# Seven-product gates in a hybrid encoder block: seven of eight feature tiles of the gate projection as 2x2 block products, the merged sum kept in fp32 and split in the w_out stage

## The chip, the core and the metric

The kernel runs on one core of a Trainium2 chip. The metric is the device time of one execution in microseconds, as a median over several runs; a second number, the span of one profiled execution with its trace, says where the time lies. The core has a matrix engine (PE, with its weight loads, PEld), a vector engine (DVE), a scalar engine (ACT), GpSimd (POOL), and SyncE (SP), which issues most of the DMAs. Each engine takes its instructions strictly in the order of its own queue, and waits for others by semaphores.

## The reference

One layer of an encoder, 512 positions of width 1024, all in float32 (cut to what matters):

```python
n = rms_norm(h, norm_mix_pre)
proj = einsum('bsd,de->bse', n, w_in)          # columns: gMLP u | v | q | k | v | gates
z_gmlp, q, k, v, gates = split(proj)
y_a = gmlp_spatial_gating(gelu(z_gmlp), ...)   # [512, 512]
y_b = mixture of three dilated window attentions(q, k, v)   # [512, 512]
g_all = sigmoid(gates + b_gate)                # gates: [512, 2048]
g_a, g_b = g_all[..., :1024], g_all[..., 1024:]
merged = g_a * (y_a @ w_branch_a) + g_b * (y_b @ w_branch_b)
h = h + rms_norm(merged @ w_out, norm_mix_post)
n2 = rms_norm(h, norm_mlp_pre)
h = h + rms_norm(square(relu(n2 @ w_up)) @ w_down, norm_mlp_post)
```

## The kernel before, in words

Every product of two float32 matrices is made of three matmuls: an operand is split into a high part (`hi`, a copy rounded by ACT into the matmul type) and a low part (`lo`, the rest, a subtraction on DVE), and `mm3` (L83-87) adds hi x hi, hi x lo and lo x hi. Such a split is `wsplit` (L70-77, ACT at L75, DVE at L76) or `split_into` (L79-81, ACT at L80, DVE at L81). A 1024x128 column block of weights is 128x1024 on the chip.

The program is a row of stages on PE: the q, k, v projections and attention of four heads; the gMLP's v and u projections (the attention of the last head, `attend(3)`, runs between them; its matmuls at L407-409 are the last readers of the split values `v0h`, `v0l`); the gates and branches (L494-514); the w_out product (L566-604); the up projection (L642-726); the down projection.

Gates and branches, before: eight feature tiles `d` of 128 columns. For each, the two gate projections are 24 matmuls of 512 columns each (8 blocks of the contraction, three matmuls each, weights x the normalised input `nh`, `nl`), a sigmoid on ACT (L506) reads each from PSUM; the two branch products are 12 matmuls of 512 columns each (`ybh`, `ybl` the attention output, `yah`, `yal` the gMLP output). DVE multiplies each with its gate (L512), adds the two (L513), and the sum is split at once into `mh` and `ml` (L514), which w_out reads. Weights come as 1 MB DMAs for two tiles (`gw`, `bw`).

The gates of the first tile run interleaved with the last attention head and the gMLP's u stage, because the scheduler that orders the instructions fills PE's queue with what it expects to be ready. The order of every engine's queue is fixed when the program is built. Buffers are taken from pools: a new tile waits for the last reader of the tile whose slot, or whose memory, it takes. PSUM has eight banks, with tags in `psA` ("acc" 4 banks, "S" 2, "T" 1, "y" 1) for the stages up to the gates and in `psB` ("acc" 4, "tp" 4) behind them; a bank of `psB` waits for the last reader of the bank of `psA` that lies there.

In the up projection the kernel already has a seven-product scheme (L654-726): two output tiles of 128 features and two halves of 256 positions form a 2x2 block product, computed with seven block products instead of eight, each of 12 matmuls of 256 columns (L687); sums of the weights (L670, L671, L676) and of the moving operand (L656-659) are made on DVE and split, and the results are put together from PSUM on DVE and ACT (L708-722).

Of the kernel before, what the change touches and what calls it, by code (L numbers as in the profile page):

```python
# [36 lines left out]
def block_kernel(ctx: ExitStack, tc: tile.TileContext, x, norm_mix_pre, w_in, b_gate, ln_v_gain, ln_v_bias,  # L37
# [157 lines left out]
    spacer(right, 160, "yedge")  # L195
# [230 lines left out]
    gpool = pool(gst, "gpool")  # L426
# [40 lines left out]

    for g2 in range(2):
# [15 lines left out]

    gst.close()
    attn.close()

    mst = ExitStack()
    mpool = pool(mst, "mpool")
    mh = mpool.tile([P, KD, S], F32R, name="mh")  # L490
    ml = mpool.tile([P, KD, S], F32R, name="ml")
    gp = ExitStack()
    gapool = pool(gp, "gapool", bufs=2)
    for d2 in range(4):  # L494
        raws = [wload([KD, 2 * P], lambda r: [(r, fcols(w_in, COL_G + br * D + d2 * 2 * P, KD, 2 * P))], "gw") for br in range(2)]
        rawb = wload([2, 4, 2 * P], lambda r: [(r[:, br], w[:, d2 * 2 * P:(d2 + 1) * 2 * P].rearrange("(k p) c -> p k c", p=P))
                                               for br, w in enumerate((w_branch_a, w_branch_b))], "bw")
        for j in range(2):
            d = 2 * d2 + j
            sl = slice(j * P, (j + 1) * P)  # L500
            tmp = []
            for br in range(2):
                wh, wl = wsplit(raws[br][:, :, sl])
                ps = feature_tile(wh, wl, KD, nhn, nln)
                sg = gapool.tile([P, S], F32, name=f"sg{br}")
                nc.scalar.activation(sg, ps, AF.Sigmoid, bias=cols[:, br * 8 + d:br * 8 + d + 1])  # L506
                tmp.append(sg)
            for br in (1, 0):
                bh, bl = wsplit(rawb[:, br, :, sl], gapool, tag=f"b{br}")
                yh, yl = ((yah, yal), (ybh, ybl))[br]  # L510
                pb = feature_tile(bh, bl, 4, yh, yl)
                nc.vector.tensor_tensor(tmp[br], pb, tmp[br], op=ALU.mult)  # L512
            nc.vector.tensor_tensor(tmp[0], tmp[0], tmp[1], op=ALU.add)  # L513
            split_into(mh[:, d], ml[:, d], tmp[0])  # L514
# [6 lines left out]
    spacer(back, 224, "nedge")  # L521
# [9 lines left out]
    KH = KD // 2  # L531
# [30 lines left out]
    def w_out_mm(t, k, hf, wh, wl):  # L562
        ts_ = slice(t * P, (t + 1) * P)
        mm3(accs[t][hf], (mh[:, k, ts_], ml[:, k, ts_]), (wh[:, halves[hf]], wl[:, halves[hf]]), k == 0, k == KD - 1)
# [44 lines left out]

    wback = pool(back, "wback", bufs=5)  # L610
# [43 lines left out]
    fe, fo = n2f[:, 0:KD:2], n2f[:, 1:KD:2]  # L654
    A, B = slice(0, 256), slice(256, 512)
    nc.vector.tensor_tensor(fe[:, :, A], fe[:, :, A], fe[:, :, B], op=ALU.subtract)  # L656
    nc.vector.tensor_tensor(fe[:, :, B], fo[:, :, B], fe[:, :, B], op=ALU.subtract)
    nc.vector.scalar_tensor_tensor(fo[:, :, B], fe[:, :, A], -1.0, fo[:, :, B], op0=ALU.mult, op1=ALU.subtract)
    nc.vector.scalar_tensor_tensor(fo[:, :, A], fo[:, :, B], -1.0, fo[:, :, A], op0=ALU.mult, op1=ALU.subtract)
    nt = {}  # L660
    for nm, src in ((2, fo[:, :, B]), (1, fe[:, :, A]), (3, fe[:, :, B]), (4, fo[:, :, A])):
        nt[nm] = (n2_tile(), n2_tile())
        split_into(*nt[nm], src)
# [3 lines left out]
    def prep(i):  # L667
        raw = raw_up(i).rearrange("p (j h) (r c) -> p j (h r) c", h=2, r=2)
        s = upool.tile([P, KH, 4, P], F32, name="s", bufs=1)
        nc.vector.tensor_tensor(s[:, :, 0:4:2], raw[:, :, 1:3], raw[:, :, 0:1].to_broadcast([P, KH, 2, P]), op=ALU.add)  # L670
        nc.vector.tensor_tensor(s[:, :, 3], s[:, :, 2], raw[:, :, 1], op=ALU.add)  # L671
        s12 = split_back(s[:, :, 2:4], [KH, 2, P])
        ar = split_back(raw[:, :, 1:3], [KH, 2, P])
        a12 = [upool.tile([P, KH, P], F32R, name="a12" + z) for z in "hl"]
        split_into(*a12, raw[:, :, 3])
        nc.vector.tensor_tensor(s[:, :, 1], s[:, :, 3], raw[:, :, 3], op=ALU.add)  # L676
        s34 = split_back(s[:, :, 0:2], [KH, 2, P])
        pick = lambda g, m: [z[:, :, m] for z in g]
        return {1: pick(ar, 0), 2: a12, 3: pick(s34, 1), 4: pick(ar, 1), 5: pick(s12, 0), 6: pick(s12, 1), 7: pick(s34, 0)}

    moving = {1: nb[0, 0], 2: nb[1, 0], 3: nb[1, 1], 4: nt[4], 5: nt[1], 6: nt[2], 7: nt[3]}

    def product(n, ps, w, first):
        (wh, wl), (bh, bl) = w[n], moving[n]
# [129 lines left out]
```

## Time and profile before

| | |
|---|---|
| median of 3 runs | 833.03 us (832.04 to 834.82) |
| profiled execution | 832.47 us |
| its span in the trace | 830.7 us, so 1.8 us lie around the span |
| PE busy | 812.6 us, 98% |
| DVE busy | 491.6 us, 59% |
| ACT busy | 348.6 us, 42% |
| gates and branches, on PE | about 306 to 432.9 us |
| w_out | 432.9 to 478.4 us |
| up projection, seven-product part | 510.3 to about 652 us |

How to read it: the page gives the busy time of each engine and the chain of work that ended last, followed back through what released each step. A timeline row has the start in us, the duration in us, the engine, the line, the operation, output and inputs by the program's names, the shape, and how many such rows in a row were put together (x2); in square brackets stands how long the engine had been idle before it, and what ended that idle time. The durations of neighbouring rows overlap by a little, since engines are pipelined; the spacing of starts is what a row costs in a dense stretch. A row of the windows table gives a stretch, its length, the busy time and number of instructions of PE, weight load, DVE, ACT and POOL, then the granted PE clock (1.00 is full), the DMA share and GB/s.

### The profile page before, as it was taken

How to read it: one execution, taken by the hardware profiler on the slowest of the kernel's cores; microseconds unless marked ns; L12 is line 12 of the kernel's file. 1: busy time of each engine (PE TensorE's matmuls, PEld its weight loads, DVE VectorE, ACT ScalarE, POOL GpSimd, SP SyncE). 2: the span in 40 equal slices, each digit the busy share in tenths (PEclk: the TensorE clock that was granted, in tenths of full speed). 3: DMA queues.
4: the chain of work that ended last, by engine and by line, in shares of the span. 5: the costliest groups of instructions: out<-in, count | busy, mean ns of one | idle time of the engine just before them, and what ended most of it. 6: DMA issues, size and time to landing. Idle time of an engine off the chain costs nothing.

```text
span 830.7 us, 10935 instructions
## 1 busy us (share of the span) xinstructions
PE 812.6 (98%) x4371; PEld 706.5 (85%) x4371; DVE 491.6 (59%) x831; ACT 348.6 (42%) x561; POOL 83.0 (10%) x81
## 2 busy tenths in 40 slices
PE   7999999999999999999999989999999999999997
PEld 5899888888888778888888879999999888888885
DVE  6422788978875647433332589989787533333324
ACT  6322243435344353332322566666666533223311
POOL 2100113232215200000000220000000000000000
PEclk9999999999999999999999989999999999999999
DMA  9433233222214134431413241443333722222202
GB/s 297 143 102 84 70 100 102 77 76 81 73 51 124 56 101 136 144 102 51 152 51 102 101 153 52 130 123 104 102 102 128 253 101 102 91 77 89 99 1 101
DMA packets 70373, 86.90 MB, mean 105 GB/s; under 512 B 2034, under 2 KB 57490, under 8 KB 70323
## 3 DMA queue, kind: packets, MB, share of 16 engines
q1 hardware_dynamic: 67810, 77.67, 29.7%
q0 software_dynamic: 2512, 8.54, 3.0%
q8 instruction: 34, 0.56, 0.3%
q14 instruction: 17, 0.13, 0.0%
HBM read 82.01 MB, written 4.19 MB: 104 GB/s over the span
## 4 chain that ended last, share of the span: by engine, by line
PE 96%; ACT 2%; DMA 1%; DVE 1%; issue 0%; SPq 0%; DVEq 0%; POOLq 0%; ACTq 0%
PE pf L87 12%; PE pf L86 11%; PE pf L85 11%; PE pacc L687 11%; PE pd L85 9%; PE pd L87 9%; PE pd L86 9%; PE ptp L687 5%; PE pv L85 4%; PE pv L86 4%; PE pv L87 4%; PE pu L85 1%; PE pu L87 1%; PE pu L86 1%; PE py L413 1%; PE psb L313 1%
## 5 line engine op out<-in xcount | busy, mean ns | idle before, releaser
L87 PE MATMUL pf<-nh,lo 128*128 128x512 f32 x352 | 138.2, 393 | 0.0
L86 PE MATMUL pf<-nl,hi 128*128 128x512 f32 x352 | 138.1, 392 | 0.0
L85 PE MATMUL pf<-nh,hi 128*128 128x512 f32 x352 | 137.8, 392 | 0.0
L687 PE MATMUL pacc<-n,hl 128*128 128x256 f32 x840 | 104.2, 279 | 0.0
L687 PEld LDWEIGHTS pacc<-n,hl 128*128 128x128 f32 x840 | 100.8, 188 | 0.3 <-ACT hl L80 0.2
L85 PE MATMUL pd<-hl,hh 128*128 128x512 f32 x224 | 87.1, 390 | 1.0 <-ACT hh L80 1.0
L86 PE MATMUL pd<-hl,hh 128*128 128x512 f32 x224 | 87.2, 389 | 0.0
L87 PE MATMUL pd<-hl 128*128 128x512 f32 x224 | 86.0, 389 | 0.0
L85 PEld LDWEIGHTS pf<-nh,hi 128*128 128x128 f32 x352 | 66.1, 188 | 13.6 <-issue 0.2
L87 PEld LDWEIGHTS pf<-nh,lo 128*128 128x128 f32 x352 | 66.1, 188 | 13.5 <-issue 0.2
L86 PEld LDWEIGHTS pf<-nl,hi 128*128 128x128 f32 x352 | 66.1, 188 | 13.3
L81 DVE TENSOR_TENSOR hl<-hid,hh 128x512 fp32r<-128x512 f32 x28 | 19.3, 693 | 80.3 <-ACT hh L80 78.9
L254 POOL TENSOR_TENSOR sw<-sw,rope 32x512 f32<-32x512 f32 x24 | 42.2, 1760 | 175.1 <-DVE sw L252 158.0
L80 ACT ACTIVATE hh<-hid 128x512 fp32r<-128x512 f32 x28 | 17.6, 631 | 93.2 <-PE pd L86 93.2
L85 PE MATMUL pv<-hi,nh 128*128 128x512 f32 x128 | 51.4, 405 | 0.9 <-ACT nh L80 0.9
L86 PE MATMUL pv<-lo,nh 128*128 128x512 f32 x128 | 51.6, 403 | 0.0
L87 PE MATMUL pv<-hi,nl 128*128 128x512 f32 x128 | 51.5, 403 | 0.0
L85 PEld LDWEIGHTS pd<-hl,hh 128*128 128x128 f32 x224 | 42.0, 188 | 10.3 <-ACT hh L80 1.4
L87 PEld LDWEIGHTS pd<-hl 128*128 128x128 f32 x224 | 42.0, 188 | 8.8
L86 PEld LDWEIGHTS pd<-hl,hh 128*128 128x128 f32 x224 | 42.0, 188 | 8.6
L81 DVE TENSOR_TENSOR hl<-dnw,hl 128x1024 fp32r<-128x1024 f32 x32 | 39.2, 1226 | 14.0 <-ACT hl L80 14.0
L75 ACT ACTIVATE hi<-qkw 128x1024 fp32r<-128x1024 f32 x24 | 25.4, 1058 | 49.3 <-PE pf L86 25.5
(246 smaller groups left out, 1557.7 us busy)
## 6 DMA issues: line engine op xcount, KB each, us to landing
upw<-in_w_up_dram SPq DMA_DIRECT2D x16, 1024.0 KB, 5.6
dnw<-in_w_down_dram SPq DMA_DIRECT2D x16, 1024.0 KB, 4.9
qkw<-in_w_in_dram SPq DMA_DIRECT2D x24, 512.0 KB, 4.4
gw<-in_w_in_dram SPq DMA_DIRECT2D x8, 1024.0 KB, 5.3
slab<-in_w_in_dram SPq DMA_DIRECT2D x6, 1024.0 KB, 12.5
wow<-in_w_out_dram SPq DMA_DIRECT2D x4, 1024.0 KB, 5.0
w0raw<-in_w_in_dram SPq DMA_DIRECT2D x4, 512.0 KB, 6.9
uw<-in_w_in_dram SPq DMA_DIRECT2D x2, 1024.0 KB, 5.7
```

The costliest lines, as they stand in the source:

```text
L75: nc.scalar.activation(hi, raw, AF.Copy)
L80: nc.scalar.activation(hi, src, AF.Copy)
L81: nc.vector.tensor_tensor(lo, src, hi.bitcast(F32), op=ALU.subtract)
L85: nc.tensor.matmul(ps, ah, bh, start=start, stop=False)
L86: nc.tensor.matmul(ps, ah, bl, start=False, stop=False)
L87: nc.tensor.matmul(ps, al, bh, start=False, stop=stop)
L254: nc.gpsimd.tensor_tensor(sw, sw, rope[:, 1], op=ALU.mult)
L313: nc.tensor.matmul(ps[:, rr, g - 1], got["q", g][:, r], got["k", g][:, r], start=True, stop=True)
L413: nc.tensor.matmul(o, v12[:, g, r, hs], ptb[r // 2][:, r % 2, g], start=False, stop=(r == 3 and g == 1), skip_group_check=True)
L687: nc.tensor.matmul(ps, a[:, j], b[:, j], start=first and not (j or m), stop=(j == KH - 1 and m == 2), skip_group_check=True)
```

## The change

`four_sums`, `seven`, `product` and `seven_pairs` are the up projection's scheme, now as functions that the gates use too (the up stage calls them with its own buffers and does what it did). For gate tile `d` the two branches' gate columns form the two rows of the block product, and the two halves of the positions its columns. Tile `d` = 0 (GSTD = 1) keeps the two standard gate products; tiles 1 to 7 use the seven products, 84 matmuls of 256 columns instead of 48 of 512. The seven-product gates need the four sums of the moving operand: `m`, a float32 tile of 8 x 512, is first filled with `nh + nl` (L555 of the changed kernel, four instructions), the sums are made in place (L476-479) and split into eight tiles `nt`. Then `m` takes the merged sums (L617), and they are split into `mhl` in the w_out stage.

The attention's pools are closed before the u stage, and `m` lies in the memory that they leave, that of `v0h`, `v0l` among it; the gMLP's buffers (`gpool`) go to the other side of the memory. Some spacers are added or moved. The buffers of the gates are single (`gs` for the two gates, `ar`, `a12`, `b0`, `b1`), the weight sums `s` share the three `raw` buffers with the weights, `gw` comes as two DMAs of 512 KB for one tile, and `bw` has two buffers of its own. The branches' products go to the PSUM tags "T" and "y" instead of "acc".

```diff
+    attn.close()
+    mst = ExitStack()
+    mpool = pool(mst, "mpool")
+    m = mpool.tile([P, KD, S], F32, name="m")
+    KH = KD // 2
+    A, B = slice(0, 256), slice(256, 512)
+
+    def four_sums(f, tiles):
+        fe, fo = f[:, 0:KD:2], f[:, 1:KD:2]
+        nc.vector.tensor_tensor(fe[:, :, A], fe[:, :, A], fe[:, :, B], op=ALU.subtract)
...
+        for nm, src in ((6, fo[:, :, B]), (5, fe[:, :, A]), (7, fe[:, :, B]), (4, fo[:, :, A])):
+            got[nm] = (tiles(), tiles())
+            split_into(*got[nm], src)
+        return got
+
+    def seven(raw, sums, split2, split1):
+        raw = raw.rearrange("p (j h) (r c) -> p j (h r) c", h=2, r=2)
+        s = sums()
+        nc.vector.tensor_tensor(s[:, :, 0:4:2], raw[:, :, 1:3], raw[:, :, 0:1].to_broadcast([P, KH, 2, P]), op=ALU.add)
+        nc.vector.tensor_tensor(s[:, :, 3], s[:, :, 2], raw[:, :, 1], op=ALU.add)
+        s12 = split2(s[:, :, 2:4], "s")
+        ar = split2(raw[:, :, 1:3], "r")
+        a12 = split1(raw[:, :, 3])
+        nc.vector.tensor_tensor(s[:, :, 1], s[:, :, 3], raw[:, :, 3], op=ALU.add)
+        s34 = split2(s[:, :, 0:2], "s")
...
+    def seven_pairs(n, weights, moving, banks, snap, rows, evac, after):
+        tail = None
+        for i in range(n):
+            c2, c1 = rows(i)
+            w = weights(i)
+            Y, Z, X = banks()
+            product(6, Y, w, moving, True)
+            if tail:
+                tail()
+            product(1, X, w, moving, True)
+            p1, z5, u2, u3 = snap("p1", 2), snap("z5", 1), snap("u2", 1), snap("u3", 1)
+            nc.scalar.activation(p1, X, AF.Copy)
+            nc.vector.tensor_tensor(u2, Y, p1, op=ALU.add)
+            product(5, Z, w, moving, True)
+            nc.scalar.activation(z5, Z, AF.Copy)
+            product(2, X, w, moving, False)
+            evac(i, c1[:, A], X)
+            product(7, Y, w, moving, False)
+            nc.vector.scalar_tensor_tensor(u3, Y, -1.0, p1, op0=ALU.mult, op1=ALU.subtract)
+            product(3, Z, w, moving, False)
+            nc.vector.tensor_tensor(c1[:, B], Z, u2, op=ALU.add)
+            nc.vector.tensor_tensor(c2[:, B], u3, z5, op=ALU.subtract)
...
+            def tail(i=i, w=w, Y=Y, p1=p1, c2=c2):
+                product(4, Y, w, moving, False)
+                nc.vector.scalar_tensor_tensor(c2[:, A], Y, -1.0, p1, op0=ALU.mult, op1=ALU.subtract)
+                after(i)
+        tail()
...
+    for k in range(0, KD, 2):
+        nc.vector.tensor_tensor(m[:, k:k + 2], nhn[:, k:k + 2].bitcast(F32), nln[:, k:k + 2].bitcast(F32), op=ALU.add)
+    nmov = four_sums(m, lambda: tpool.tile([P, KH, 256], F32R, name="nt", tag="nt"))
...
-    mh = mpool.tile([P, KD, S], F32R, name="mh")
-    ml = mpool.tile([P, KD, S], F32R, name="ml")
...
+    def gate_banks():
+        return [psA.tile([P, 512], F32, name="pg" + tag, tag=tag, bufs=nb)[:, A] for tag, nb in (("acc", 4), ("acc", 4), ("S", 2))]
+
+    def gate_evac(i, dst, X):
+        d = i + GSTD
+        nc.scalar.activation(dst, X, AF.Sigmoid, bias=cols[:, d:d + 1])
+
+    def gate_after(i):
+        d = i + GSTD
+        nc.scalar.activation(gs[d][:, 1, B], gs[d][:, 1, B], AF.Sigmoid, bias=cols[:, d:d + 1])
+        nc.scalar.activation(gs[d][:, 0], gs[d][:, 0], AF.Sigmoid, bias=cols[:, 8 + d:9 + d])
+        branches(d)
+
+    def branches(d):
+        g = gs.pop(d)
+        for br in (1, 0):
+            bhl = gapool.tile([P, 2, 4, P], F32R, name=f"b{br}")
+            split_into(bhl[:, 0], bhl[:, 1], rawb[d][:, br])
+            yh, yl = ((yah, yal), (ybh, ybl))[br]
+            pb = feature_tile(bhl[:, 0], bhl[:, 1], 4, yh, yl, "Ty"[br])
+            nc.vector.tensor_tensor(g[:, 1 - br], pb, g[:, 1 - br], op=ALU.mult)
+        nc.vector.tensor_tensor(m[:, d], g[:, 0], g[:, 1], op=ALU.add)
...
-            split_into(mh[:, d], ml[:, d], tmp[0])
...
+    mhl = []
+    for k in range(KD):
+        hl = n2pool.tile([P, 2, S], F32R, name="mhl", tag="n2")
+        split_into(hl[:, 0], hl[:, 1], m[:, k])
+        mhl.append(hl)
```

How the queues change, at the two places that the prediction speaks of. In the rows that follow, a row is an instruction with its line, output, inputs and shape; x3 stands for three in a row, and the brackets name the engines or DMAs whose semaphores it waits for.

DVE before, from the end of the last attention head on (`ybl` is its output's low part, `sv` the gMLP's gated values, `bw` the branch weights):

```order
L76 TENSOR_TENSOR lo<-gw,hi 128x1024 [waits DVE_49,DMAHW7_49,PE_49,Activation_49]
L81 TENSOR_TENSOR ybl<-py,ybh 128x512 [waits Activation_49]
L76 TENSOR_TENSOR lo<-bw,hi 128x512 [waits DMAHW6_49,Activation_49]
L480 SCALAR_TENSOR_TENSOR sv<-pg,cols,sbias 128x512 [waits DVE_49,PE_49]
L480 SCALAR_TENSOR_TENSOR sv<-pg,cols,sbias 128x512 [waits DVE_49]
L76 TENSOR_TENSOR lo<-bw,hi 128x512 [waits DMAHW5_49,DVE_49,Activation_49]
```

DVE in the changed kernel at the same place (`s` are weight sums, `m` the sums of the moving operand, `nt` their split halves):

```order
L76 TENSOR_TENSOR lo<-s,hi 128x1024 [waits PE_49,Activation_49]
L555 TENSOR_TENSOR m<-nh,nl 128x1024 [waits PE_49]
L555 TENSOR_TENSOR m<-nh,nl 128x1024 x3
L81 TENSOR_TENSOR ybl<-py,ybh 128x512 [waits Activation_49]
L476 TENSOR_TENSOR m<-m 128x4x256 [waits DVE_49]
L477 TENSOR_TENSOR m<-m 128x4x256 [waits DVE_49]
L549 SCALAR_TENSOR_TENSOR sv<-pg,cols,sbias 128x512 [waits PE_49]
L549 SCALAR_TENSOR_TENSOR sv<-pg,cols,sbias 128x512
L478 SCALAR_TENSOR_TENSOR m<-m 128x4x256 [waits DVE_49]
L551 SCALAR_TENSOR_TENSOR sv<-sv,u 128x512 [waits DVE_49] x2
L479 SCALAR_TENSOR_TENSOR m<-m 128x4x256 [waits DVE_49]
```

The eight instructions on `m` have come in here, and the next rows are a step of the gelu (L451) and the first of the four low parts `nt` (L81); PE's queue has the seven products of tile 1 behind the gMLP's `pg` matmuls, and the branches of tile 0 further on.

ACT in the changed kernel, behind the high parts of `nt` (`hi_2898` belongs to the weight sums of tile 2, `gs_2664` is the pair of gates of tile 0, `pf_2675` and `pf_2705` its two PSUM banks):

```order
L75 ACTIVATE hi_2898<-s_2884 128x1024 [waits PE_49,Activation_49]
L80 ACTIVATE yah_2171<-sv_2581 128x512 [waits DVE_49]
L80 ACTIVATE yah_2171<-sv_2626 128x512 [waits DVE_49]
L624 ACT_TABLE_LOAD
L624 ACTIVATE gs_2664<-pf_2675,cols_65 128x512 [waits Activation_49]
L624 ACTIVATE gs_2664<-pf_2705,cols_65 128x512
L80 ACTIVATE ar_2780<-gw_2767 128x1024 [waits DMAHW6_49,DMAHW5_49]
```

Before, the table load and the two sigmoids of tile 0 stood right behind `ybh`, ahead of the four splits of `bw` and of all four `yah`; now they stand behind the four high parts of `nt`, a weight split that waits for PE, and the last `yah`.

DVE before, at the end of the gates (`pf_3452` is the PSUM bank of the last branch product, `wow` are w_out's weights):

```order
L512 TENSOR_TENSOR sg0_3397<-pf_3452,sg0_3397 128x512 [waits PE_49]
L513 TENSOR_TENSOR sg0_3397<-sg0_3397,sg1_3428 128x512 [waits DVE_49]
L81 TENSOR_TENSOR ml_2629<-sg0_3397,mh_2628 128x512 [waits Activation_49]
L76 TENSOR_TENSOR lo_3636<-wow_3633,hi_3635 128x1024 [waits DMAHW5_49,Activation_49]
L76 TENSOR_TENSOR lo_3640<-wow_3633,hi_3639 128x1024 [waits DMASW5_49,DMASW6_49,DMASW4_49,DMASW7_49,DMASW0_49,Activation_49]
```

DVE in the changed kernel, at the end of the gates (`pgacc_3707` is the bank of product 4 of tile 7, `pf_3861` that of its last branch product, with tag "y"):

```order
L530 SCALAR_TENSOR_TENSOR gs_3682<-pgacc_3707,p1_3784 128x256 [waits PE_49]
L81 TENSOR_TENSOR mhl_3936<-m_2438,mhl_3936 128x512 [waits Activation_49]
L76 TENSOR_TENSOR lo_4023<-wow_4020,hi_4022 128x1024 [waits DMAHW4_49,Activation_49]
L76 TENSOR_TENSOR lo_4081<-wow_4078,hi_4080 128x1024 [waits DMAHW5_49,Activation_49]
L76 TENSOR_TENSOR lo_4085<-wow_4078,hi_4084 128x1024 [waits Activation_49]
L76 TENSOR_TENSOR lo_4091<-wow_4088,hi_4090 128x1024 [waits DMAHW6_49,Activation_49]
L76 TENSOR_TENSOR lo_4095<-wow_4088,hi_4094 128x1024 [waits Activation_49]
L616 TENSOR_TENSOR gs_3682<-pf_3861,gs_3682 128x512 [waits Activation_49]
```

The multiplication that reads the last branch bank now stands behind five weight splits of w_out. On ACT, behind the last sigmoid that reads PSUM (L601), stand seven high parts of `mhl` and the five of `wow`, and then the sigmoid (L606) that this multiplication waits for.

PE in the changed kernel at the same place, the last rows of product 4 and the first of w_out (`pd_3954` is the first bank of `psB`):

```order
L503 MATMUL pgacc_3707<-nt_2652,ar_3696 128x256
L503 MATMUL pgacc_3707<-nt_2651,ar_3696 128x256
L85 MATMUL pd_3954<-hi_3964,mhl_3918 128x512 [waits DVE_49]
L86 MATMUL pd_3954<-lo_3965,mhl_3918 128x512
L87 MATMUL pd_3954<-hi_3964,mhl_3918 128x512
```

Before, the first w_out matmul came right behind the last branch matmul and waited for PE alone; now it waits for DVE, since `pd_3954` lies in the bank of `pf_3861`, which L616 reads.

174 lines of the change are left out of this document (79 added, 95 removed).

## The prediction, made before the changed kernel was run

> **What bounds the kernel now.** First the page: the span, the engines' busy shares, and the chain that ended last.
>
> ```profile
> span 830.7 us, 10935 instructions
> PE 812.6 (98%) x4371; PEld 706.5 (85%) x4371; DVE 491.6 (59%) x831; ACT 348.6 (42%) x561; POOL 83.0 (10%) x81
> PE 96%; ACT 2%; DMA 1%; DVE 1%; issue 0%; SPq 0%; DVEq 0%; POOLq 0%; ACTq 0%
> ```
>
> PE is the bound nearly everywhere, so fewer matmuls save time as long as PE has the next one ready; the other engines matter only where PE waits. So the trace has to answer three things: what a 512-wide and a 256-wide matmul cost, whether DVE and ACT can feed the new scheme, and what PE does at the two seams, into the gates and out of them. The chain in order of time gives the first (start, length, step):
>
> ```profile
> 345.68 0.24 PE pf L86
> 362.22 0.24 PE pf L86
> ...
> 482.63 1.90 ACT hl L80 x2
> 484.58 0.58 PE pu L85
> 510.26 1.40 PE pacc L687 x12
> ```
>
> Between the first two rows lies one feature tile of 72 matmuls: 16.54 us, so 0.2297 us for each 512-wide one. In the up stage 12 matmuls 256 wide take 1.40 us, 0.1167 each: half the width costs just over half.
>
> **The saving.** Seven tiles go from 48 x 0.2297 = 11.03 us of gate matmuls to 84 x 0.1167 = 9.80: 1.23 us each, **-8.6 us**. [...]
>
> **Can DVE and ACT keep up?** The windows table for the up stage's seven products (start:end, length, then busy time of PE, PEld, DVE, ACT, POOL), then from the groups by line inside it the mean ns of one, and the page's row for the gate weights (us to landing):
>
> ```profile
> 510.00:652.00 142.00, 141.79 (x1196) 140.64 (x1195) 119.48 (x171) 91.46 (x128) 2.69 (x5) 1.00 0.40 125
> ```
>
> ```profile
> L687 PEld LDWEIGHTS pacc<-n,hl 128*128 128x128 f32 x840 | 100.8, 188 | 0.3 <-ACT hl L80 0.2
> L81 DVE TENSOR_TENSOR hl<-s,hl 128x1024 fp32r<-128x1024 f32 x27 | 33.0, 1221 | 6.7 <-ACT hl L80 6.7
> L80 ACT ACTIVATE hl<-s 128x1024 fp32r<-128x1024 f32 x26 | 27.5, 1059 | 28.9 <-DVE s L671 14.2 <-DVE s L676 9.5 <-PE pacc L687 5.0
> L676 DVE TENSOR_TENSOR s<-s,upw 128x512 f32<-128x512 f32 x13 | 8.9, 684 | 0.1
> L717 DVE TENSOR_TENSOR hid<-pacc,u 128x256 f32<-128x256 f32 x14 | 5.9, 421 | 1.5 <-PE pacc L687 1.4
> L708 ACT ACTIVATE p<-ptp 128x256 f32<-128x256 f32 x14 | 5.3, 378 | 4.0 <-PE ptp L687 3.5
> ```
>
> ```profile
> gw<-in_w_in_dram SPq DMA_DIRECT2D x8, 1024.0 KB, 5.3
> ```
>
> A new tile on PE is 9.80 + 24 x 0.2297 = 15.3 us. On DVE it needs four 128x1024 (one sum, three splits, 4.9 us), eight 128x512 (two sums, a split, two branch splits, two products, the merged sum, 5.5) and five 128x256 results (2.1): 12.5 us. ACT has three 128x1024, five or six half as long, and four small: under 8. The up stage runs with DVE busy for 119.48 of 142 us, 84%, and PE at 141.79, so 12.5 of 15.3 (82%) hides in the same way. What the deletions release, the `mh`/`ml` split of 0.69 on DVE per tile, only moves. The single buffers and the 512 KB DMAs I price at 0 to 1.5 us in all: each weight tile has a whole tile of time ahead of its use, against 5.3 us of landing on the page; without that cover a tile would lose 1 to 2 us. I take 0.
>
> **Seam one, into the gates.** `m` lies where `v0` was, so its first instruction waits for attend(3) to finish, and DVE is in order. The timelines of DVE, ACT and PE around it:
>
> ```profile
> 302.57 1.23 DVE L76 TENSOR_TENSOR lo<-gw,hi 128x1024 fp32r<-128x1024 f32 x1 [4.08 <-ACT hi L75]
> 306.24 0.69 DVE L81 TENSOR_TENSOR ybl<-py,ybh 128x512 fp32r<-128x512 f32 x1 [2.45 <-ACT ybh L80]
> 309.95 1.41 DVE L480 SCALAR_TENSOR_TENSOR sv<-pg,cols,sbias 128x512 f32<-128x512 f32 x2
> 311.27 1.28 DVE L76 TENSOR_TENSOR lo<-bw,hi 128x512 fp32r<-128x512 f32 x2
> 437.00 3.50 DVE L76 TENSOR_TENSOR lo<-wow,hi 128x1024 fp32r<-128x1024 f32 x3 [1.13 <-ACT hi L75]
> ```
>
> ```profile
> 306.23 1.28 ACT L506 ACT_TABLE_LOAD   x1
> 307.52 1.27 ACT L506 ACTIVATE sg<-pf,cols 128x512 f32<-128x512 f32 x2
> 308.68 2.19 ACT L75 ACTIVATE hi<-bw 128x512 fp32r<-128x512 f32 x4
> ```
>
> ```profile
> 302.49 0.28 PE L409 MATMUL py<-ptah,v0l 128*128 128x256 f32 x1
> ...
> 305.41 1.06 PE L478 MATMUL pg<-wst,vln 128*128 128x128 f32 x8
> 306.99 1.16 PE L478 MATMUL pg<-wst,vln 128*128 128x128 f32 x8 [0.52 <-DVE ybl L81]
> 309.36 0.49 PE L85 MATMUL pf<-ybh,hi 128*128 128x512 f32 x1 [1.21 <-ACT hi L75]
> ```
>
> In a row a 128x1024 costs DVE 1.14 us (3.50 for three, the last one whole), a 128x512 0.60 to 0.66 (1.28 and 1.41 for two). The last reader of `v0` ends at 302.77; the split at 302.57 leaves DVE free at 303.7. Then, in the order shown with the change, by the times of before's trace: four instructions on `m` to 308.3, `ybl` 308.9, L476 and L477 311.2, two `sv` 312.5, L478 313.7, two gated values 314.9, L479 and a gelu step 316.7, the first `nt` low part 317.9. Product 6 of tile 1 needs it, and PE has nothing ahead of that but `pg` matmuls (0.87 us for eight, until 306.28, and some 2.6 us more); the branches of tile 0 stand further on. Products 6 and 5 then cost 2.8 us. Product 6 of tile 2 takes the PSUM bank of tile 0's first gate, whose sigmoid now stands on ACT behind the last gMLP splits: DVE does four more splits (`yal`, `nt`) and two `sv` to 324.3, the weight split 325.5, two gated values 326.7; ACT the last `yah` 327.4, table load 328.7, sigmoid 329.3. So PE has real work again at **329.4**. From 306.28 that is 23.1 us with 2.6 + 2.8 of work: 17.7 idle, against 0.52 + 1.21 there before: **+16.0**. For a shorter value: if `m` were not waited for, PE would go on at about 312, a cost near 0; for a longer one, tile 0's branch weights are queued on SP behind a load that waits for that weight split, which makes 2 to 3 us more. I take 16.
>
> **The clock.** Idle PE costs twice. In the windows around w_out's end PE was nearly idle from 478.4 to 484.6:
>
> ```profile
> 482.00:484.00 2.00, 0.44 (x2) 0.37 (x2) 2.00 (x6) 2.00 (x4) 0.68 (x2) 0.75 0.39 156
> 488.00:490.00 2.00, 2.00 (x12) 2.00 (x12) 0.79 (x2) 2.00 (x4) 0.00 (x0) 0.55 0.91 298
> 490.00:492.00 2.00, 2.00 (x20) 2.00 (x18) 2.00 (x2) 1.01 (x2) 0.00 (x0) 1.00 0.48 166
> 654.00:656.00 2.00, 1.01 (x4) 0.86 (x5) 1.76 (x3) 2.00 (x4) 0.00 (x0) 1.00 0.68 223
> ```
>
> ```profile
> 477.97 0.40 PE L87 MATMUL pd<-hi,ml 128*128 128x512 f32 x1
> 486.03 0.41 PE L85 MATMUL pu<-n,hl 128*128 128x256 f32 x1
> 489.23 0.41 PE L85 MATMUL pu<-n,hl 128*128 128x256 f32 x1
> ```
>
> The granted clock, the last column but two, falls to half at about 483 (0.75 from 482 to 484) and is back at about 489.8 (0.55 from 488 to 490), 5.2 us after work began at 484.6, and 15 matmuls 256 wide take 3.20 us, 0.213 each. So a restart loses 5.2 x (1 - 0.1167/0.213) = 2.35 us; an idle microsecond (654 to 656) costs no clock. Both seams idle for over 7 us: **+2.35 each**. [...]
>
> **Seam two, into w_out.** ACT's row for the splits of `wow`, and PE's first matmul of w_out:
>
> ```profile
> 435.91 4.85 ACT L75 ACTIVATE hi<-wow 128x1024 fp32r<-128x1024 f32 x5 [0.76 <-DVE ml L81]
> ```
>
> ```profile
> 432.86 0.40 PE L85 MATMUL pd<-hi,mh 128*128 128x512 f32 x1
> ```
>
> Before, PE went from the last branch straight on at 432.86, since the `wow` splits came later. Now the first w_out matmul waits for L616 on bank "y", which DVE reaches only after `mhl` and five weight splits. From the end of product 2 of tile 7: sigmoid 0.4, seven `mhl` high parts at 0.55 (2.19 for four) 3.8 in all, the first `wow` high part 1.06, five low parts 5.8, L616 0.7, hops between engines 0.2 by estimate: 12.0 us. In that time PE does products 7 and 4, 2.8 us. **+9.2** idle, some 1 us of it ahead of product 4, which waits for L523 among the `mhl` splits. The low bound is 2 us (the mere turnaround of a sigmoid, L616 and a hop, as if nothing were queued ahead); the high one 12, if the last `wow` load came late.
>
> **Behind it.** The chain has the split of the first up weights (1.90 us at 482.63) ahead of the up stage; in the changed order these splits are issued earlier: -1 (from -2 to +1). The up stage's code only moved into functions, and the down stage's not at all: 0.
>
> **The sum.** -8.6 + 16.0 + 2.35 + 9.2 + 2.35 - 1 = +20.3 on the profiled execution of 832.47, **852.8**; that execution lies 0.6 below the median, so against the median 853.3. I say 853. With seam one at 13 to 19 (3 us either way for times carried over into another order), seam two at 6 to 12 (less is the rival in which it does not stall) and the step behind it at -2 to 1, this case spans 846 to 861.
>
> **The rivals.** *The stalls are filled, faster* (0.05): `m` gets its turn while PE has other ready work, and the bank is free in time; then only the saving stands, with 1 or 2 us of turnaround: 825. It decides if PE restarts by about 312 at seam one and within 2 us at seam two. For it: DVE is 59% busy in all. Against: both queues are in order, and what stands ahead is work, not waiting.
>
> *Only seam one stalls* (0.08): w_out's bank or weights come as before. 852.8 - 9.2 - 2.35 = 841. *Only seam two* (0.04): 852.8 - 16.0 - 2.35 = 834.5, within 0.3% of before; it needs `m` summed by 306, against the split at 302.57 ahead of it.
>
> *The tiles stall as well* (0.13): with single buffers, product 6 of the next tile waits for a weight split that waits for a buffer, 1 to 2 us per tile: 860 to 867. For it: in the up stage ACT already sat idle 28.9 us waiting for sums. Against: PE there waited 0.2 us of 142.
>
> *256-wide matmuls cost more in the gates than in the up stage* (0.01): if their spacing fell to the weight load's 0.188 us, 84 x (0.188 - 0.1167) = 6 us more for each of seven tiles, 895. Against: the up stage's 0.1167 has the same loads, which overlap there. [...]
>
> That the change does not do what it says is no case: the queue holds 84 matmuls of 256 columns per tile.
>
> **Chances.** The forecast 0.69, the rivals as given. What a measurement of this kernel can tell from no change is about 0.3%, 2.5 us. Faster 0.05, same 0.04, slower 0.91. The range goes from 841 (seam one alone) to 862 (a little of the stalling tiles); outside lie the fast rivals and the worst stalls.
>
> **What would show it.** In the changed profile: PE idle of about 12 us up to product 6 of tile 1 (released by DVE `nt`) and about 8 up to product 6 of tile 2 (released by ACT's sigmoid), about 8 ahead of the first `pd` (released by DVE L616), a granted clock of 0.5 for some 5 us behind each, and a dense 15.3 us per tile between. It is wrong if PE is dense through either seam, or if tiles take over 16 us.

## The result and the profile after

| | before | after |
|---|---|---|
| median of 6 runs | 832.56 us (831.89 to 834.82) | 855.33 us (853.32 to 857.31) |
| ratio, 95% interval | | 1.0269 (1.0249 to 1.0289) |
| profiled execution | 832.47 us | 853.32 us |
| span | 830.7 us | 851.5 us |

The changed kernel is 22.8 us slower in the median; the two profiled executions differ by 20.9 us (the profiled one of after is the fastest of its six). The page of after, its rows of busy time and of the chain:

```profile
PE 811.8 (95%) x4623; PEld 717.6 (84%) x4623; DVE 546.5 (64%) x913; ACT 370.3 (43%) x600; POOL 82.1 (10%) x82
PE 89%; DVE 5%; DMA 2%; ACT 1%; issue 1%; SPq 0%; DVEq 0%; POOLq 0%; ACTq 0%
```

PE is busy for as long as before (811.8 against 812.6 us), in a span that is 20.8 us longer: the matmul time that was saved came back as idle time and as matmuls at half clock (mean granted clock 0.982, before 0.994). In the chain PE fell from 96% to 89%, and DVE rose from 1% to 5%.

**The dense stretch.** Between the seams PE ran without a gap, up to 434.44. Two rows of PE's timeline, the first matmul of product 2 (the weights `a` belong to it), three tiles apart, and the window of one tile:

```profile
378.30 0.28 PE L503 MATMUL pgS<-nh,a 128*128 128x256 f32 x1
...
424.68 0.28 PE L503 MATMUL pgS<-nh,a 128*128 128x256 f32 x1
```

```profile
345.00:360.30 15.30, 15.30 (x108) 14.28 (x107) 10.20 (x15) 6.17 (x10) 0.00 (x0) 1.00 0.41 107
```

(424.68 - 378.30)/3 = 15.46 us per tile against 16.53 before (five tiles from 344.58 to 427.25 by the starts of their branches in its timeline), PE never idle, DVE busy for 10.20 us of 15.3. From the restart at 329.33 to 434.44 no row of PE's timeline shows idle time. Seven tiles save 7.5 us.

**Seam one.** PE's timeline of after, only the rows ahead of which it was idle:

```profile
308.89 2.07 PE L547 MATMUL pg<-wst,vln 128*128 128x128 f32 x8 [2.52 <-DVE ybl L81]
311.94 3.60 PE L547 MATMUL pg<-wst,vln 128*128 128x128 f32 x16 [0.98 <-DVE sv L549]
316.29 0.38 PE L503 MATMUL pgacc<-nt,hi 128*128 128x256 f32 x1 [0.63 <-ACT nt L80]
317.80 0.39 PE L503 MATMUL pgacc<-nt,hi 128*128 128x256 f32 x1 [1.13 <-DVE nt L81]
320.14 0.58 PE L503 MATMUL pgacc<-nt,hi 128*128 128x256 f32 x1 [0.29 <-DVE nt L81]
329.33 0.79 PE L503 MATMUL pgacc<-nt,hi 128*128 128x256 f32 x2 [6.79 <-ACT gs L624]
```

DVE and ACT at the same place:

```profile
303.61 4.62 DVE L555 TENSOR_TENSOR m<-nh,nl 128x1024 f32<-128x1024 f32 x4
...
314.80 1.21 DVE L479 SCALAR_TENSOR_TENSOR m<-m 128x1024 f32<-128x1024 f32 x1
...
316.53 1.21 DVE L81 TENSOR_TENSOR nt<-m,nt 128x1024 fp32r<-128x1024 f32 x1
...
326.70 1.30 DVE L81 TENSOR_TENSOR yal<-sv,yah 128x512 fp32r<-128x512 f32 x2
```

```profile
326.04 1.23 ACT L80 ACTIVATE yah<-sv 128x512 fp32r<-128x512 f32 x2 [2.46 <-DVE sv L551]
327.29 1.28 ACT L624 ACT_TABLE_LOAD   x1
328.59 1.27 ACT L624 ACTIVATE gs<-pf,cols 128x512 f32<-128x512 f32 x2
```

From 303.61 to 328.0 DVE has no gap: the sums on `m`, then sums, gMLP steps and splits by turns. Until the sigmoid at 328.59 frees the bank, PE gets only short pieces of work, and from 308.38 on most of it at half clock (granted 0.50; the steps are shown further below): the 24 `pg` matmuls at 308.89 and 311.94 take 2.07 + 3.60 = 5.7 us.

**Seam two.** PE, then DVE, then ACT of after:

```profile
442.31 1.68 PE L503 MATMUL pgacc<-nt,ar 128*128 128x256 f32 x12 [0.81 <-DVE u L523]
452.86 0.80 PE L85 MATMUL pd<-hi,mhl 128*128 128x512 f32 x1 [8.87 <-DVE gs L616]
```

```profile
446.45 5.75 DVE L76 TENSOR_TENSOR lo<-wow,hi 128x1024 fp32r<-128x1024 f32 x5
452.13 0.68 DVE L616 TENSOR_TENSOR gs<-pf,gs 128x512 f32<-128x512 f32 x1
```

```profile
444.14 4.83 ACT L75 ACTIVATE hi<-wow 128x1024 fp32r<-128x1024 f32 x5
448.88 0.71 ACT L606 ACTIVATE gs<-gs,cols 128x512 f32<-128x512 f32 x1
```

The multiplication that PE waits for takes 0.68 us; it stands behind 5.75 us of weight splits, and its sigmoid behind 4.83.

**The ledger at the first `pd`**, which came at 452.86 instead of 432.86, 20.0 us later: tiles -7.5; restart at seam one 329.33, +16.0 by the prediction's reckoning; 2.9 us at half clock behind it, by an estimate from the 0.1167 and 0.213 us of the prediction's rows +1.3; seam two 8.87 + 0.81, and 0.75 that PE stood idle at 434.44 for the low part `ar`, +10.4. Sum +20.2. From there on: w_out takes 47.21 us from its first `pd` to the end of its last (counted as 0.23 us), against 45.34, +1.9; from there to the first `pacc` 30.9 against 31.9, -1.0; the rest is equal within 0.1.

### The profile page after: what moved, and what is told of

Same layout as the page of the kernel before. It is cut to its first block, busy times and chain, and to the rows that moved or that the text cites. A ratio compares the mean times of both kernels' runs of the same rounds, so it can differ in the third digit from the quotient of the medians.

```text
span 851.5 us, 11623 instructions
## 1 busy us (share of the span) xinstructions
PE 811.8 (95%) x4623; PEld 717.6 (84%) x4623; DVE 546.5 (64%) x913; ACT 370.3 (43%) x600; POOL 82.1 (10%) x82
## 4 chain that ended last, share of the span: by engine, by line
PE 89%; DVE 5%; DMA 2%; ACT 1%; issue 1%; SPq 0%; DVEq 0%; POOLq 0%; ACTq 0%
PE pacc L503 12%; PE pf L86 8%; PE pf L85 8%; PE pf L87 8%; PE pd L85 8%; PE pd L87 8%; PE pd L86 8%; PE pgacc L503 5%; PE ptp L503 5%; PE pv L85 4%; PE pv L87 4%; PE pv L86 4%; PE pgS L503 2%; DMA h<-in_x_dram 1%; PE pu L86 1%
## 5 line engine op out<-in xcount | busy, mean ns | idle before, releaser
L87 PE MATMUL pf<-nh,lo 128*128 128x512 f32 x240 | 94.6, 394 | 0.0
L86 PE MATMUL pf<-nl,hi 128*128 128x512 f32 x240 | 94.4, 393 | 0.0
L85 PE MATMUL pf<-nh,hi 128*128 128x512 f32 x240 | 94.1, 393 | 0.0
L81 DVE TENSOR_TENSOR hl<-hid,hh 128x512 fp32r<-128x512 f32 x28 | 19.3, 693 | 80.4 <-ACT hh L80 78.9
L85 PEld LDWEIGHTS pf<-nh,hi 128*128 128x128 f32 x240 | 45.1, 188 | 9.1 <-issue 0.2
L87 PEld LDWEIGHTS pf<-nh,lo 128*128 128x128 f32 x240 | 45.1, 188 | 9.0 <-issue 0.2
L86 PEld LDWEIGHTS pf<-nl,hi 128*128 128x128 f32 x240 | 45.1, 188 | 8.9
L81 DVE TENSOR_TENSOR hl<-dnw,hl 128x1024 fp32r<-128x1024 f32 x32 | 39.2, 1225 | 13.8 <-ACT hl L80 13.8
```

Source lines behind the costliest of these rows:

```text
L81: nc.vector.tensor_tensor(lo, src, hi.bitcast(F32), op=ALU.subtract)
L85: nc.tensor.matmul(ps, ah, bh, start=start, stop=False)
L86: nc.tensor.matmul(ps, ah, bl, start=False, stop=False)
L87: nc.tensor.matmul(ps, al, bh, start=False, stop=stop)
```

## The experiments

The theory: two separate stalls, each a queue of work in front of one instruction, and a price for the clock behind each. The first rival: the late instruction isn't the cause, and PE would wait for something else. `issue_after(x)` in the diffs puts the instructions inside behind `x` in their queues. A comparison "from the first `pg`" counts from the start of the gMLP's first `pg` matmul, because the executions reach that point up to 2.8 us apart even where nothing ahead of it differs.

**e1, splits behind the last gate.** For `mhl` of tiles 2 to 6, five of the eight, and the last four splits of `wow`; `sigs[-1]` is the last gate's sigmoid, `ends[-1]` the last merged sum:

```diff
+            with tc.issue_after(sigs[-1]), tc.issue_after(ends[-1]):
                 split_into(hl[:, 0], hl[:, 1], m[:, k])
```

> The changed kernel with six of the eight splits of the merged sum (k = 2 to 6) and the last four splits of w_out's weights queued behind the last gate's sigmoid and sum; no work is added or left out. My theory (the first w_out matmul waits for the multiplication that empties bank y, and that one only stands behind splits which nobody needs yet): product 4 of the last tile starts some 0.7 us earlier, the first w_out matmul comes about 2 us behind product 4 instead of 8.9, the clock stays full, so 7.7 + 2.35 = 10 us less than the changed kernel's 855.3: about 845, ratio to before 1.015. Rival (the splits have to be done anyway and w_out only waits for them later, or the bank is not what is waited for): no gain, 853 to 856.

Measured 849.42 us (ratio 1.0185, 1.0155 to 1.0214). PE's timeline and the window behind:

```profile
446.14 0.50 PE L85 MATMUL pd<-hi,mhl 128*128 128x512 f32 x1 [2.20 <-DVE gs L616]
```

```profile
446.14:452.00 5.86, 5.86 (x26) 4.84 (x27) 5.86 (x8) 5.86 (x9) 0.00 (x0) 1.00 0.66 239
496.10:502.90 6.80, 4.17 (x20) 4.07 (x20) 5.75 (x11) 3.19 (x7) 2.58 (x2) 0.50 0.20 80
```

The stall went from 8.87 to 2.20 us, and the clock stayed at 1.00: the order of the queues is what made seam two. The profiled execution gained 7.7 us; the median gained 5.9, less than the 10 expected. In the trace the clock now fell at the next gap, between w_out and the up stage (0.50 from 496.1 to 502.9), where it had stayed at 1.00 in after (499.54 to 506.36, shown further below).

**e2, the clock alone.** 26 matmuls of 512 columns without use, into a bank that is overwritten later, keep PE busy ahead of w_out:

```diff
+    for i in range(26):
+        nc.tensor.matmul(accs[3][1], mhl[0][:, 0, :P], mhl[0][:, 0], start=True, stop=True)
```

> The changed kernel with 26 extra matmuls of 512 columns in the idle stretch ahead of w_out, into a bank that w_out fills afresh later; they cost nothing on the path, since PE idles there. My theory (a restart after the idle stretch runs at half clock for over 5 us and costs 2.35 us): the first w_out matmul still comes at about 452.9 in the trace but at full clock, total 2.35 us less than 855.3: 853. [...] Rival (the slow start is not the idle time's doing): no change, 855.3, or up to 2 us more if the extra matmuls run into w_out.

Measured 855.62 us (1.0271, 1.0246 to 1.0296): no gain.

```profile
445.41 6.07 PE L683 MATMUL pd<-mhl 128*128 128x512 f32 x26
454.45 0.50 PE L85 MATMUL pd<-hi,mhl 128*128 128x512 f32 x1 [2.97 <-DVE gs L616]
```

```profile
454.45:460.00 5.55, 5.55 (x24) 4.61 (x25) 1.36 (x2) 0.63 (x1) 0.00 (x0) 1.00 0.67 189
```

w_out ran at full clock and took 44.56 us instead of 47.21: the price of the half clock there is 2.65 us. The total does not show it. This execution came into the gates 1.6 us later (first `pg` at 306.91, in after 305.31), which lies ahead of the added matmuls and is not their doing; and the clock fell at the start of the up stage, as in e1 (0.50 from 508 to 510), so that the way from w_out's end to the first `pacc` took 32.4 us, in after 30.9.

**e3 and e4, more tiles in the usual form.** GSTD = 2 and 3, so that PE has ready gate matmuls for seam one:

```diff
-    GSTD = 1
+    GSTD = 2
```

> The changed kernel with two standard gate tiles instead of one (GSTD = 2), so six with seven products. My theory (at seam one PE has nothing ready while DVE makes the sums): the 48 matmuls of tile 1 are ready there and fill 11.0 of the 17.7 idle us; the saving of one tile, 1.23, is lost: 855.3 - 11.0 + 1.2 = 845.5, and 2 less if the clock stays full. Rival (seam one's length is set by a chain that starts later when PE does other work first): 856.5, the loss of one tile's saving alone.

> The same with three standard tiles (GSTD = 3), five with seven products. My theory: 22 us of ready matmuls cover all 17.7 idle us of seam one and its half clock, two tiles' saving is lost: 855.3 - 16.0 - 2.35 + 2.5 = 839.5. Rival (filler only moves the wait): 857.8.

Measured 857.22 us (1.0289, 1.0267 to 1.0311) and 860.81 us (1.0327, 1.0302 to 1.0352): my expectation fell. The rival's number held in e3 (856.5), and e4 came out 3 us above it (857.8). PE of e3, DVE of e3, PE of e4:

```profile
340.27 0.80 PE L503 MATMUL pgacc<-nt,hi 128*128 128x256 f32 x2 [15.34 <-ACT gs L624]
```

```profile
310.82 1.23 DVE L76 TENSOR_TENSOR lo<-s,hi 128x1024 fp32r<-128x1024 f32 x1 [5.41 <-ACT hi L75]
...
314.67 4.62 DVE L555 TENSOR_TENSOR m<-nh,nl 128x1024 f32<-128x1024 f32 x4
```

```profile
339.99 0.79 PE L85 MATMUL pf<-nh,hi 128*128 128x512 f32 x1 [14.72 <-ACT gs L624]
```

The scheduler put nearly all the added matmuls ahead of the end of attend(3), where PE had no need of them. The sums on `m` began at 314.67 instead of 303.61, though in e3 the last reader of `v0` had started at 305.23: on DVE a weight split stood ahead of them, which waited until 310.82 for its high part, and three weight sums behind it. The whole seam slid: from the first `pg` to the restart 340.27 - 316.50 = 23.8 us, in after 329.33 - 305.31 = 24.0. In e4 it is a plain 512-wide gate matmul that waits for tile 0's sigmoid, so the wait belongs to the bank, not to the seven products. Why does that sigmoid stand so late? `gs`, which it writes, is allocated in the memory of the gMLP's buffers, so it must come behind their last reader, the last `yah` and `yal`. The prediction saw the place in the queue, not this reason.

**e5, `gs` in memory of its own**, which the attention has left:

```diff
+    gspool = pool(gp, "gspool")
     tpool = pool(gp, "tpool", bufs=8)
...
-        gs[d] = gapool.tile([P, 2, S], F32, name="gs")
+        gs[d] = gspool.tile([P, 2, S], F32, name="gs")
```

> The changed kernel with the gates' tile gs in a pool of its own that lies over the attention's memory instead of over the gMLP's; nothing else differs. The two sigmoids of tile 0 then stand right behind ybh on ACT, as before the change, and the bank of its first gate is free by about 309. My theory now (two waits in a row make seam one: DVE's sums hold product 6 of tile 1 until 317.8, the sigmoid holds product 6 of tile 2 until 329.3; and the sigmoid is that late because gs lies over the gMLP's buffers): products 6 and 5 of tile 2, 2.8 us, move ahead into the idle stretch, and PE then waits for the weight split ar, which stands behind the same gMLP splits, to about 329: 2 to 3 less than 855.3, about 852.5. Rival (the bank's sigmoid is all that PE waits for): PE goes on from 321.6, 7.7 less or more, 846 to 848.

Measured 849.95 us (1.0198, 1.0182 to 1.0214). ACT and PE:

```profile
309.61 1.26 ACT L625 ACTIVATE gs<-pf,cols 128x512 f32<-128x512 f32 x2
...
328.83 0.63 ACT L80 ACTIVATE yah<-sv 128x512 fp32r<-128x512 f32 x1 [1.11 <-DVE sv L552]
329.37 1.04 ACT L80 ACTIVATE ar<-gw 128x1024 fp32r<-128x1024 f32 x1
```

```profile
330.46 0.58 PE L503 MATMUL pgS<-nh,ar 128*128 128x256 f32 x1 [5.07 <-ACT ar L80]
...
448.42 0.68 PE L85 MATMUL pd<-hi,mhl 128*128 128x512 f32 x1 [4.34 <-DVE gs L617]
```

The sigmoid came 19 us earlier, and the bank held nobody up. But after products 6 and 5 of tile 2, which now ran earlier, PE stood still again until 330.46: the next thing in line, the split `ar` of tile 1's weights, stands on ACT behind the same last `yah`, which waits for the same DVE. What seam one gained is read at a place that both queues share: product 4 of tile 7 starts 442.41 - 307.50 = 134.9 us after the first `pg`, in after 442.31 - 305.31 = 137.0, so 2.1 us, as my theory had it (2 to 3). The time of 849.95 lies between the two expectations all the same, because most of the gain came from seam two, where the new buffer changed the order as well: one `wow` split ahead of the last multiplication instead of five, 4.34 us idle instead of 8.87.

**e6, the filler where it is needed.** e5 with GSTD = 2, and tile 1's gate matmuls behind the last matmul of the attention:

```diff
+            with tc.issue_after(pys[-1 if d else 0]):
+                ps = feature_tile(*w, KD, nhn, nln)
```

> e5 with two standard tiles, the 48 gate matmuls of tile 1 queued on PE behind the last attention head's matmuls. In e3 they ran ahead of them, and DVE's sums, which wait for that head, started 11 us later. My theory (PE idles because nothing ready stands in its queue while DVE works from 303.6 to 328): the same 11.0 us of matmuls now lie inside DVE's chain: 855.3 - 11.0 + 1.2 = 845.5. Rival (as e3: filler only moves the wait): 857.

Measured 848.41 us (1.0176, 1.016 to 1.0192).

```profile
336.88 0.58 PE L504 MATMUL pgS<-nh,ar 128*128 128x256 f32 x1 [11.33 <-ACT ar L80]
```

Now PE ran without a gap from its first `pg` to 325.5, and then stood still for 11.33 us in one piece, since DVE, busy from 304.78 to 336.6 but for 1.6 us, had more weight sums and splits to do besides the sums on `m`. Product 4 of tile 7 started 441.35 - 307.62 = 133.7 us after the first `pg`, 1.2 us sooner than in e5. With the 1.1 us that this tile no longer saves, about 2.3 of the 11 us of filler were of use. A filler mostly delays the wait if it brings work for the engine that is late.

**e7, the sums left out.** The eight tiles `nt` are then made of `nh` as it is.

```diff
-    for k in range(0, KD, 2):
+    for k in ():
         nc.vector.tensor_tensor(m[:, k:k + 2], nhn[:, k:k + 2].bitcast(F32), nln[:, k:k + 2].bitcast(F32), op=ALU.add)
-    nmov = four_sums(m, lambda: tpool.tile([P, KH, 256], F32R, name="nt", tag="nt"))
+    nmov = four_sums(nhn.bitcast(F32), lambda: tpool.tile([P, KH, 256], F32R, name="nt", tag="nt"), False)
...
-        nc.vector.tensor_tensor(fe[:, :, A], fe[:, :, A], fe[:, :, B], op=ALU.subtract)
...
+        if summed:
+            nc.vector.tensor_tensor(fe[:, :, A], fe[:, :, A], fe[:, :, B], op=ALU.subtract)
```

> The changed kernel with the sums of the moving operand left out: the four L555 and the four of L476-479 are gone, the eight tiles nt are made of nh as it is, so the gates' values are not the reference's; all matmuls and splits stay. My theory (DVE's chain of sums, splits and gMLP steps sets when PE goes on): eight instructions of 1.14 to 1.2 us, 9.3 us, leave the chain, and the splits no longer wait for v0: 9.3 less than 855.3, 846; 2 less again if the clock stays full. Rival (the sums are hidden behind another wait, the sigmoid's or the weights'): 853 to 856.

Measured 850.44 us (1.02, 1.0183 to 1.0218).

```profile
324.18 0.79 PE L504 MATMUL pgacc<-nt,hi 128*128 128x256 f32 x2 [10.00 <-ACT gs L625]
```

From the first `pg` to the restart 324.18 - 306.48 = 17.7 us instead of 24.0: the sums, some 9.4 us of DVE (L555 4.62, four sums of about 1.2), are worth 6.3 of seam one's 16. The total gained 4.9 us, less than the 9.3 expected, for what still held PE was the order behind the sums: in this trace DVE works from 308.25 to 322.85 without a gap on gMLP steps, `nt` splits and a weight split, and the bank's sigmoid comes behind the last of them. That remainder was not taken apart further.

**e8 and e10, no seven products in the gates.** GSTD = 8 and no sums, and so no buffers for `nt`; all else of the change stays (merged sum in fp32, split in w_out; single buffers of `gs`, `b0`, `b1`; 512 KB loads; banks "T" and "y"):

```diff
-    for k in range(0, KD, 2):
+    for k in ():
         nc.vector.tensor_tensor(m[:, k:k + 2], nhn[:, k:k + 2].bitcast(F32), nln[:, k:k + 2].bitcast(F32), op=ALU.add)
-    nmov = four_sums(m, lambda: tpool.tile([P, KH, 256], F32R, name="nt", tag="nt"))
...
-    GSTD = 1
+    GSTD = 8
...
-    seven_pairs(KD - GSTD, gate_weights, nmov, gate_banks, lambda nm, nb: gapool.tile([P, 256], F32, name=nm, bufs=nb),
-                gate_rows, gate_evac, gate_after)
```

> The changed kernel with all eight tiles' gates as two standard products (48 matmuls of 512 columns each), no sums and no seven-product tiles; the merged sum in fp32, its splits in the w_out stage, the buffers and the DMAs of the change stay. My theory (the cost comes from the sums at seam one and from what stands ahead of the last bank at seam two, not from keeping the merged sum in fp32): PE is dense through seam one, and w_out's first matmul waits 1.5 to 2 us for the last sum: 833 + 1.5 = 834.5, ratio 1.002. Rival (the split in the w_out stage costs the 9 us at seam two with any gates, or the smaller DMAs and single buffers cost): 842 to 845.

> The kernel of e8 (all eight tiles with 48 matmuls of 512 columns, no sums; the rest of the change stays), five rounds, to tell whether its 0.9967 of the time before is real. If the rest of the change is worth the 3 us by which the first pd came earlier, the ratio is again 0.995 to 0.998, about 830 us; rival: it is no difference, 0.999 to 1.001.

Measured 830.22 us (0.9967, 0.9939 to 0.9995), and again, in eight runs against thirteen of before, 830.18 us (0.9968, 0.9955 to 0.998). PE's timeline of e10:

```profile
317.17 0.50 PE L85 MATMUL pf<-nh,hi 128*128 128x512 f32 x1 [0.87 <-ACT gs L620]
...
429.49 0.50 PE L85 MATMUL pd<-hi,mhl 128*128 128x512 f32 x1 [0.49 <-ACT mhl L80]
```

This version is faster than both, by 0.3% against before, in two sets of runs, and below the 834.5 that my theory gave. Both seams are gone with the seven products, so the fp32 sum, the splits in w_out and these buffers cost nothing in sum: w_out's bank and splits are no obstacle where DVE comes to the end of the gates with nothing in arrears.

**e9, e6 and e1 together.**

> e6 and the late splits of e1 in one kernel (gates in their own memory, two tiles in the usual form with tile 1's gate matmuls behind the attention, and the splits of mhl and wow queued behind the last gate). Theory that the two seams are separate causes, but that e5's changed order has already taken part of what the late splits give: e6's first pd stood idle 4.33 us, e1's 2.20, so 2.1 us less than e6's 848.4: 846. Rival that the gains simply add (e6 848.4 less e1's 5.9): 842.5. In either case it stays above 832.6, since DVE's chain at the first seam is untouched.

Measured 844.02 us (1.013, 1.0104 to 1.0157), with its first `pd` after 2.20 us idle as in e1, and an 11.32 us stall at seam one as in e6. That lies between the two expectations (846 and 842.5), so it doesn't tell them apart; four runs spread from 841.2 to 847.4. The best that I made of the seven-product gates is still 11 us slower than before.

## Why the prediction was right, point by point

- **The forecast** was 852.8 us for the profiled execution, measured 853.3, and 853 for the median, measured 855.3. Part of that closeness is luck: the profiled execution is the fastest of its six, and of the terms the saving and seam two came out some 1.1 us dearer each, the clock at seam one about as much cheaper.
- **The signs.** The places and releasers of the waits came out as said: `nt` low part at 317.80 (317.9 was said), restart at 329.33 (329.4), released by ACT's sigmoid; the first `pd` by DVE L616. The size of the first did not: up to product 6 of tile 1 PE was idle for 2.52 + 0.98 + 0.63 + 1.13 = 5.3 us, not about 12, and up to product 6 of tile 2 for 6.8, not 8. The prediction priced the work inside the seam at full clock (2.6 us for the `pg` matmuls, which took 5.7). DVE's queue sets the restart, so the slower matmuls only filled the wait.
- **The saving** was mis-sized by 1.1 us: a tile takes 15.46 us, not 15.3, for 84 matmuls of 256 columns cost 0.119 each here (with 24 branch matmuls at 0.229), while the up stage's twelve showed 0.1167; and before, a tile took 16.53.
- **DVE and ACT keep up** in the dense stretch, with more to spare than said (10.2 us in a window of 15.3, said 12.5).
- **Single buffers and 512 KB loads at 0**: the dense tiles bear that out up to tile 7, where PE stood 0.75 us for the single `ar`; e8 and e10 bear it out for the loads and for `gs`, `b0` and `b1`.
- **Seam one at +16.0** was right, but its reason was cut short. The prediction took the place of the sigmoid from the queue; e4 and e5 showed that the memory of `gs` put it there, and that taking that away gives only 2.1 us, because the next wait stands behind the same work on DVE. e7 is the nearest to the cause: remove DVE's sums, and 6.3 of the 16 us go.
- **Seam two at +9.2** was 10.4, with 0.75 of the difference on a low part that `ar` needed in the last tile. The rest is DVE's own arrears: the prediction let the five low parts follow ACT's first high part of `wow`, ready at 444.14 + 1.06 = 445.20, but DVE, without a gap from 440.63 on, came to them at 446.45. The prediction's 0.2 us for hops between engines stands on no row; the last of them, from the end of L616 (452.13 + 0.68) to the first `pd` at 452.86, took 0.05. e1 shows the cause as it was named: queue order.
- **The clock at 2.35 for each seam** was mis-sized too: 1.3 at seam one, 2.65 at seam two (e2). The 5.2 us of half clock behind a restart, read from one place, is no constant; and even there PE's timeline of before has the first matmul behind the gap at 483.63, not 484.6, so 6.2 us. Windows of after, cut at the points where the granted clock (last column but two) changes:

```profile
308.38:311.79 3.41, 2.07 (x8) 1.78 (x8) 3.38 (x4) 0.00 (x0) 0.00 (x0) 0.50 0.00 0
311.79:315.21 3.42, 3.27 (x15) 3.27 (x16) 3.42 (x6) 1.50 (x3) 0.00 (x0) 0.50 0.00 0
315.21:318.62 3.41, 1.65 (x12) 1.25 (x12) 3.41 (x5) 3.41 (x5) 0.00 (x0) 1.00 0.02 5
...
328.86:332.27 3.41, 2.94 (x14) 2.94 (x14) 1.44 (x2) 2.73 (x5) 0.00 (x0) 0.50 1.19 291
332.27:335.69 3.42, 3.42 (x27) 3.25 (x26) 2.60 (x4) 1.26 (x2) 0.00 (x0) 1.00 0.61 145
```

```profile
441.50:444.92 3.42, 1.68 (x13) 1.48 (x12) 3.42 (x8) 3.42 (x7) 0.63 (x2) 1.00 0.00 0
...
451.74:455.16 3.42, 2.30 (x5) 1.82 (x6) 2.45 (x4) 0.63 (x1) 0.14 (x1) 0.50 0.50 123
455.16:458.57 3.41, 3.41 (x9) 2.64 (x8) 0.00 (x0) 0.00 (x0) 0.00 (x0) 0.50 0.54 184
```

Between 303 and 462 us of the trace the clock changes eight times, at 308.38, 315.21, 318.62, 322.03, 325.45, 332.27, 448.33 and 458.57: all on a grid of 3.413 us (44 steps from the first to the last). PE restarted 0.47 us into a step at seam one and worked for 2.94 of its 3.41 us; the clock was 1.00 from the next step on, 2.9 us after the restart. At seam two it restarted 1.1 us into a step and worked for 2.30 of its 3.42 us; the clock was 0.50 in the next step too, and back at 1.00 only 5.7 us after the restart.
- **"Behind it" at -1** had the right size (-1.0 from w_out's end to the first `pacc`) and the wrong reason. The earlier splits of the up weights gained nothing: PE's idle time there is 4.0 us in before and 4.5 in after. What differs most is the clock. Of before, after and e1, in steps of the grid:

```profile
479.57:482.98 3.41, 1.27 (x8) 0.84 (x8) 3.41 (x7) 3.41 (x9) 1.17 (x3) 1.00 0.03 10
482.98:486.39 3.41, 2.61 (x10) 2.32 (x11) 3.41 (x7) 2.06 (x3) 2.49 (x1) 0.50 0.38 154
```

```profile
499.54:502.95 3.41, 1.86 (x12) 1.06 (x10) 3.31 (x10) 3.41 (x9) 2.22 (x4) 1.00 0.53 189
502.95:506.36 3.41, 2.01 (x12) 1.38 (x12) 3.32 (x6) 3.16 (x8) 0.00 (x1) 1.00 0.31 119
```

```profile
492.68:496.10 3.42, 1.91 (x12) 1.37 (x12) 3.18 (x7) 3.25 (x6) 0.83 (x2) 1.00 0.49 164
```

In before the clock was 0.50 behind a step with 1.27 us of work, for 6.2 us, which by an estimate from the 0.213 and 0.1167 us of the prediction's rows cost 2.8 us; in after each step held 1.85 us or more, and it stayed at 1.00. In e1 and e2 it fell again (0.50 from 496.1 to 502.9 and from 508 to 510), and the same way took 32.9 and 32.4 us. Of the 2.8, 0.5 went to the longer idle time and about 0.8 to eight transposes (a row x8 of `pt`) that in before ran inside w_out; 0.5 stays open. How much work keeps the clock is not settled by PE's busy time alone: after kept it behind the step with 1.68 us at 441.50, and e1 lost it behind the one with 1.91. That the same kernel draws it in one execution and not in the next, by where the grid lies, is only argued: the other five executions of after, up to 4 us longer, have no trace. Their mean granted clock on record is 0.976 to 0.981, against 0.982 of the profiled one, which fits, though not in proportion to their times.
- **The rivals**: neither seam was missing, no tile stalled but the last by 0.75 us, and the 256-wide matmuls kept their spacing within 2%. That the stalls could be filled was tried in e3, e4, e6 and e9; the nearest, e9, is 11 us above the time before.

## What to carry to other kernels

A scheme that spares PE 1.1 us per tile must first be charged with what it adds at the two ends of its stage, in series, on the engines that feed it: here 9.4 us of sums ahead of the gMLP's last steps, and splits ahead of one short multiplication. Look there for what memory and banks a new tile takes over, because that fixes its place in the queue; and when one wait is removed, ask what else stands behind the same engine. Then run the change without its main idea: here that was the one that gained.

## What the runs showed of the hardware that was not expected

- In the stretches shown the granted clock changes only on a 3.413 us grid (after, eight changes from 308.38 to 458.57). Behind steps with 1.27 us of PE work (before, 479.57) and 1.65 (after, 315.21) the clock fell to 0.50; behind steps with 1.68 (after, 441.50; it was still 1.00 from 444.92 to 448.33) and 1.86 (after, 499.54) it stayed at 1.00, but in e1 it fell behind one with 1.91 (492.68), so PE's busy time gives no sharp border. At 0.50 it came back to 1.00 behind steps with 2.94 us of work (after, 328.86) and 3.27 (311.79), and stayed at 0.50 behind steps with 2.07 (308.38), 2.30 (451.74) and 2.61 (before, 482.98).
- Branch matmuls of the same shape were closer together in e10 than before, with the clock at 1.00 in both (from 346 to 426). Before, then e10, the first branch matmul of a tile and the first gate matmul of the next:

```profile
361.12 0.40 PE L85 MATMUL pf<-ybh,hi 128*128 128x512 f32 x1
...
366.73 0.40 PE L85 MATMUL pf<-nh,hi 128*128 128x512 f32 x1
```

```profile
358.11 0.39 PE L85 MATMUL pf<-ybh,b 128*128 128x512 f32 x1
...
363.55 0.39 PE L85 MATMUL pf<-nh,hi 128*128 128x512 f32 x1
```

24 matmuls take 5.61 us before and 5.44 in e10, 0.234 against 0.227 each; over eight tiles that is 1.4 of the 2.8 us which e10 gains. Its branch weights lie in one tile of high and low parts instead of two. Whether that is the cause wasn't tried.
